# One pass over four heads for the state space products of a two-layer hybrid decoder kernel

## The chip, the cores and the metric

The kernel runs on one core of a Trainium2 chip. The metric is the device time of one execution in microseconds (us). The kernel before was timed in three runs: 1581.88, 1584.16 and 1584.36 us, median 1584.16 us. A separate, profiled execution took 1581.26 us.

## What is computed

Two decoder layers over 272 tokens (16 learned meta tokens, then 256) of width 2048. Each layer normalises its input, projects it once to all branch inputs, runs three branches (attention, a pooling mixer, and the state space part) and projects their outputs back. The part that the change touches is the chunked state space product of the reference:

```
cb = jnp.einsum('bclgn,bcsgn->bcgls', cm, bm)
y_diag = jnp.einsum('bcgrls,bcsgrp->bclgrp', cb[:, :, :, None] * lm, xdt)
...
y_off = jnp.einsum('bclgn,bcgrpn,bcgrl->bclgrp', cm, prev, jnp.exp(cs))
return (y_diag + y_off).reshape(b, tp, h, p)
...
y = y + d_skip.astype(jnp.float32)[:, None] * xs
yg = (y.reshape(b, t, SSD_WIDTH) * jax.nn.silu(z.astype(jnp.float32))).reshape(b, t, SSD_GROUPS, -1)
```

There are 32 heads of 64 channels in 4 groups of 8, and two chunks of 128 tokens besides the 16 meta tokens. `y_diag` is the product within a chunk (the chunk product), `y_off` what comes from the state ahead of the chunk (the state product).

## The kernel before, in words

Channels lie on partitions and tokens along the free dimension, so a tile holds 128 channels by 272 tokens. The large projections are done as three fp32r matmuls each (lines 244 to 246): weights are split into a high half `wh` (ScalarE, line 211) and a rest `wl` (VectorE, line 219), up to ten half tiles ahead of TensorE. One column block of 256 outputs is 96 such matmuls, in four quarters of 24.

All other work is written as generators that a `tick()` after each quarter moves on by one step. So the order of every engine's instructions is fixed when the program is built: the step of a generator lies on TensorE between two quarters of a projection. A `yield` puts off what follows by one quarter, and `until(key)` waits (while building) for another generator to have come past a point. The engines then run their queues in this order and wait for each other through semaphores alone.

The state space part goes group by group. The blocks of a group are `xs` (two of them), `BC`, and `z` (two of them). For each group:

- `post_xs` (two blocks of 256 channels): VectorE takes the projection out of PSUM (line 459, into `xpad`), ScalarE and VectorE do the convolution (lines 796 and 802), ScalarE the silu (806) and copies of the meta tokens (`xr`, 826), then TensorE transposes (`px`, lines 845 and 847) and VectorE and GpSimd scale (852, 855, 860) and ScalarE and VectorE split (864, 865).
- `post_BC` makes `H`, the state ahead of each chunk, and starts four `decay` generators. Each fills `M` for one pair of heads (the masked product of `cb` and `lm`; VectorE 935, ScalarE 941, GpSimd 948).
- `post_z` runs once for each z block, that is, for two pairs of heads (four heads). It takes the gate out of PSUM, waits for `M` of a pair `c`, yields once, and calls `ssd_y` for that pair; then the same for the second pair. After a further step VectorE adds and gates (988, 990), ScalarE squares (992), GpSimd sums (993, 1001 to 1003), TensorE sums over partitions (`pn`, 1007), VectorE and GpSimd make the root (1010 and `rsqrt_g`, lines 272 to 282), VectorE scales (1015) and the mix is split.
- `ssd_y` does one pair of heads. In layer 0 alone there are two 16-token matmuls for the meta tokens (961). Then come four chunk products, two heads by two chunks, with 64 columns of weights each, the two heads to the two halves of PSUM's partitions (966, `py`). Then two state products of 128 columns, one for each chunk (970, `ph`). VectorE scales `ph` into `yo` (972) and adds the skip term to `py` (973).

Layer 1 drops the meta tokens here (`t0` is 16), so it has no line 961.

The bank ring `aux` has four PSUM banks. `py` and `ph` take one bank each for every pair of heads.

The lines around the call, in `post_z`:

```
for c in (2 * j, 2 * j + 1):
    yield from until(f"M{g}_{c}")
    yield 1
    yo = yo or pair("yo")
    ssd_y(g, c, yo)
yield 1
```

Of the kernel before, what the change touches and what calls it, by code (L numbers as in the profile page):

```python
# [13 lines left out]
OP = mybir.AluOpType  # L14
# [4 lines left out]
P = 128  # L19
T = 272  # L20
# [8 lines left out]
PRE, POST, CW, CB, NW, PSC, DSK = 0, 16, 32, 128, 152, 168, 176  # L29
# [73 lines left out]
def hybrid(ctx: ExitStack, tc: tile.TileContext, I, out, dbg=None, layers=2):  # L103
# [15 lines left out]
    V, A, G, TE = nc.vector, nc.scalar, nc.gpsimd, nc.tensor  # L119

    def pair(name):
        return pr.tile([P, 2, T], F32, name=name, tag="pair")

    def aux(name):
        return psa.tile([P, 512], F32, name=name, tag="a")
# [36 lines left out]
    for l in range(layers):  # L162
# [10 lines left out]
        for i in range(4):  # L173

            if i < 3:
                j = seq.index(("i", l, [b[:2] for b in blocks].index(("pv", i + 1)), PLQ))
            else:
                j = seq.index(("o", l, 0, PLQ))
            seq.insert(j + 1, ("p", l, i, 0))

    hseq, j = [], 0
    while j < len(seq):
        n = 1 + NLEAD if seq[j][:2] == ("m", 0) else 1
# [86 lines left out]
    def rsqrt_g(y, v, t):  # L270

        G.tensor_scalar(y.bitcast(I32), v.bitcast(I32), -0.5, RSQ, op0=OP.mult, op1=OP.add)
        G.tensor_tensor(t, y, y, op=OP.mult)
        G.tensor_tensor(t, t, v, op=OP.mult)
        G.tensor_scalar(t, t, -1.0, K2, op0=OP.mult, op1=OP.add)
        G.tensor_tensor(y, y, t, op=OP.mult)
        G.tensor_tensor(t, y, y, op=OP.mult)
        G.tensor_tensor(v, t, v, op=OP.mult)
        G.tensor_scalar(t, v, K1 ** 4, -10.0 / 3 * K1 * K1, op0=OP.mult, op1=OP.add)
        G.tensor_tensor(t, t, v, op=OP.mult)  # L280
        G.tensor_scalar(t, t, KF, 5.0 * KF, op0=OP.mult, op1=OP.add)
        G.tensor_tensor(y, y, t, op=OP.mult)
# [72 lines left out]
    def layer(L, hs):  # L355
        t0 = 0 if L == 0 else NM
        last = L == layers - 1
        TQ = T - t0
        pa = par[:, L]
# [7 lines left out]
        def until(key):  # L367
            while key not in done:
                yield 1
# [84 lines left out]
        def dump_m(name, ap):  # L454
            if name in dbg:
                nc.gpsimd.dma_start(dbg[name][:, :, t0:], ap[:, :, t0:])
# [102 lines left out]
        def mix_out(mix, f, c0, n):  # L559

            m, c = mix
            A.copy(m[:, 0, c:c + n, c0:T], f)
            V.tensor_tensor(m[:, 1, c:c + n, c0:T], f, m[:, 0, c:c + n, c0:T].bitcast(F32), op=OP.subtract)
# [206 lines left out]
        def gate(ps, c0, key):  # L770
            g_ = pair("gate")
            evac_r(g_[:, :, c0:T], ps, 2, c0)
            done.add(("ev",) + key)
            yield 1
            A.activation(g_[:, :, c0:T], g_[:, :, c0:T], AF.Silu)
            yield 1
            return g_
# [173 lines left out]
                                op=OP.mult)  # L951
            done.add(f"M{g}_{c}")

        def ssd_y(g, c, yo):
            s = sd[g]
            M, H, csb, xdt, cT = s["M"], s["H"], s["csb"], s["xdt"], s["C"]
            py = aux("py")
            if t0 == 0:
                for j in range(2):
                    h = 2 * c + j  # L960
                    TE.matmul(py[64 * j:64 * j + 64, 0:16], xdt[0:16, 0, h], M[0:16, h, 0:16], start=True, stop=True)
            for b in range(2):
                sl = slice(16 + b * P, 144 + b * P)
                for j in range(2):
                    h = 2 * c + j
                    TE.matmul(py[64 * j:64 * j + 64, sl], xdt[:, 1 + b, h], M[:, h, sl], start=True, stop=True)
            ph = aux("ph")
            for b in range(2):
                sl = slice(16 + b * P, 144 + b * P)
                TE.matmul(ph[:, sl], H[:, b, 2 * c:2 * c + 2].rearrange("p h d -> p (h d)"), cT[:, sl],  # L970
                          start=True, stop=True)
            V.tensor_tensor(yo[:, c % 2, 16:], ph[:, 16:T], csb[:, 2 * c, 16:], op=OP.mult)
            V.scalar_tensor_tensor(s["yg"][:, c, t0:], s["x"][c // 2][:, c % 2, t0:],
                                   pa[:, DSK + 4 * g + c:DSK + 4 * g + c + 1], py[:, t0:T], op0=OP.mult, op1=OP.add)

        def post_z(i, ps):
            g, j = i // 2, i % 2
            zg = yield from gate(ps, t0, ("z", i))
            s = sd[g]
            yg = s["yg"]  # L980
            yo = None
            for c in (2 * j, 2 * j + 1):
                yield from until(f"M{g}_{c}")
                yield 1
                yo = yo or pair("yo")
                ssd_y(g, c, yo)
            yield 1
            V.tensor_tensor(yg[:, 2 * j:2 * j + 2, 16:], yg[:, 2 * j:2 * j + 2, 16:], yo[:, :, 16:], op=OP.add)
            ysl = yg[:, 2 * j:2 * j + 2, t0:]
            V.tensor_tensor(ysl, ysl, zg[:, :, t0:T], op=OP.mult)  # L990
            q = pair("ysq")
            A.activation(q[:, :, t0:], ysl, AF.Square)
            G.tensor_tensor(q[:, 0, t0:], q[:, 0, t0:], q[:, 1, t0:], op=OP.add)  # L993
            if j == 0:
                s["q"] = q
                done.add(f"q{g}")
                return
            done.add(f"y{g}")
            yield from until(f"q{g}")
            qs = pr.tile([P, 2, T], F32R, name="ysr", tag="pair")  # L1000
            G.tensor_tensor(qs[:, 0, t0:], q[:, 0, t0:], s["q"][:, 0, t0:], op=OP.add)
            G.tensor_tensor(q[:, 0, t0:], q[:, 0, t0:], s["q"][:, 0, t0:], op=OP.add)
            G.tensor_tensor(qs[:, 1, t0:], q[:, 0, t0:], qs[:, 0, t0:].bitcast(F32), op=OP.subtract)
            yield PNY
            pn = aux("pn")
            for k in range(2):
                TE.matmul(pn[:, t0:T], ones_r, qs[:, k, t0:], start=k == 0, stop=k == 1)
            yield 1
            v = s["q"][:, 0, t0:]
            V.tensor_scalar(v, pn[:, t0:T], 1.0 / 512, EPS, op0=OP.mult, op1=OP.add)  # L1010
            rg = q[:, 0, t0:]
            rsqrt_g(rg, v, q[:, 1, t0:])
            yield PGY
            for c in range(4):
                V.scalar_tensor_tensor(yg[:, c, t0:], yg[:, c, t0:], pa[:, NW + 4 * g + c:NW + 4 * g + c + 1], rg,
                                       op0=OP.mult, op1=OP.mult)
            dump_m(f"mixS{L}_{g}", yg)
            m = slots.tile([P, 2, 4, T], F32R, name=f"mixS{L}_{g}", tag=f"S{SS[g]}")
            mixS[g] = m
            yield 1  # L1020
            mix_out((m, 0), yg[:, :, t0:], t0, 4)
            done.add(f"mixS{g}")
# [50 lines left out]
        def post_pg(i, ps):  # L1073
# [6 lines left out]
            for c in range(2):  # L1080
# [5 lines left out]

        post = {"iq": post_iq, "k": post_k, "v": post_v, "q": post_q, "ag": post_ag,
                "xs": post_xs, "BC": post_BC, "z": post_z, "pv": post_pv, "pg": post_pg}

        def banks(ps):  # L1090
# [342 lines left out]
    h = hs  # L1433
    for L in range(layers):
        h = layer(L, h)
# [78 lines left out]
```

## Time and profile before

| | |
|---|---|
| profiled execution | 1581.26 us |
| its span in the trace | 1579.5 us |
| median of the three timed runs | 1584.16 us |
| TensorE (matmul) busy | 1540.3 us, 98% |
| VectorE busy | 1206.4 us, 76% |
| ScalarE busy | 884.6 us, 56% |
| GpSimd busy | 416.5 us, 26% |

The span runs from the first to the last instruction of the program; the execution's own time is 1.8 us more than it. A busy share is a share of the span. In the trace every fp32 matmul stands as two records (two passes); a fp32r matmul is one. Matmuls overlap in the pipeline, so what one costs TensorE is the distance from its start to the next start, not its duration.

### The profile page before, as it was taken

The numbers are of one execution on the slowest core, as the hardware profiler recorded it, in microseconds if no ns is written. First come the engines' busy times: TensorE is split into PE (matmuls) and PEld (weight loads), VectorE is DVE, ScalarE is ACT, GpSimd is POOL, SyncE is SP. The second block draws the span as 40 slices with busy tenths as digits, with TensorE's granted clock in tenths as the row PEclk, the third lists the DMA queues.
The fourth block names the chain that finished last, engine by engine and source line by source line (L and its number), as shares of the span: only waits on it lengthen the run. The fifth ranks groups of instructions, "written<-read, shape, count | busy, mean of one in ns | idle before, by whom it ended". The sixth has DMA issues, their size and how long they took to land. (4 is left out here: it accounts for less than half of the span.)

```text
span 1579.5 us, 31128 instructions
## 1 busy us (share of the span) xinstructions
PE 1540.3 (98%) x11788; PEld 1475.4 (93%) x11788; DVE 1206.4 (76%) x2217; ACT 884.6 (56%) x1663; POOL 416.5 (26%) x416
## 2 busy tenths in 40 slices
PE   7999999999999999999998999999999999999997
PEld 6899999999999999999998999999999999988886
DVE  7899777798989776545588998787989888764554
ACT  6455566656667444444455555666676565444542
POOL 3823342233342421000103314322333324200000
PEclk9999999999999999999999999999999999999999
DMA  6545445454544465565536454454545455566652
GB/s 232 204 146 174 138 135 180 143 189 136 188 172 154 130 207 169 191 217 176 171 108 230 152 173 157 149 188 148 197 153 181 174 162 164 190 225 207 208 188 93
DMA packets 78310, 272.44 MB, mean 172 GB/s; under 512 B 8848, under 2 KB 11984, under 8 KB 77136
## 3 DMA queue, kind: packets, MB, share of 16 engines
q1 hardware_dynamic: 78064, 270.39, 51.5%
q8 instruction: 92, 1.51, 0.4%
q14 instruction: 58, 0.48, 0.1%
q10 hardware_dynamic: 96, 0.07, 0.0%
HBM read 266.03 MB, written 4.40 MB: 171 GB/s over the span
## 5 line engine op out<-in xcount | busy, mean ns | idle before, releaser
L219 DVE TENSOR_TENSOR wl<-wr,wh 128x512 fp32r<-128x512 f32 (+1 forms) x952 | 712.7, 773 | 270.0 <-PE go L246 70.5
L211 ACT CAST wh<-wr 128x512 fp32r<-128x512 f32 (+1 forms) x952 | 564.6, 615 | 430.2 <-PE go L245 91.7
L244 PE MATMUL g0xs<-u,wh 128*128 128x272 f32 x256 | 74.8, 292 | 0.0
L244 PE MATMUL g1xs<-u,wh 128*128 128x272 f32 x256 | 74.6, 291 | 0.0
L244 PE MATMUL g0z<-u,wh 128*128 128x272 f32 x256 | 74.5, 291 | 0.0
L246 PE MATMUL go<-mixS,wl 128*128 128x272 f32 x256 | 74.1, 290 | 0.0
L246 PE MATMUL g0xs<-u,wl 128*128 128x272 f32 x256 | 74.1, 290 | 0.0
L246 PE MATMUL g0z<-u,wl 128*128 128x272 f32 x256 | 74.1, 290 | 0.0
L246 PE MATMUL g1xs<-u,wl 128*128 128x272 f32 x256 | 74.1, 289 | 0.0
L244 PE MATMUL go<-mixS,wh 128*128 128x272 f32 x256 | 74.0, 289 | 0.0
L245 PE MATMUL g1xs<-u,wh 128*128 128x272 f32 x256 | 73.7, 288 | 0.0
L245 PE MATMUL g0xs<-u,wh 128*128 128x272 f32 x256 | 73.7, 288 | 0.0
L245 PE MATMUL g0z<-u,wh 128*128 128x272 f32 x256 | 73.6, 288 | 0.0
L245 PE MATMUL go<-mixS,wh 128*128 128x272 f32 x256 | 73.6, 288 | 0.0
L244 PE MATMUL g1z<-u,wh 128*128 128x256 f32 x256 | 72.7, 284 | 0.0
L451 POOL TENSOR_TENSOR ropet<-ropet,rope 128x512 f32<-128x512 f32 (+2 forms) x20 | 33.2, 1661 | 147.7 <-PE ptr L483 66.1
L246 PE MATMUL g1z<-u,wl 128*128 128x256 f32 x256 | 71.7, 280 | 0.0
L245 PE MATMUL g1z<-u,wh 128*128 128x256 f32 x256 | 71.6, 280 | 0.0
L948 POOL TENSOR_TENSOR M<-M,cbm 128x512 f32<-128x512 f32 x32 | 45.9, 1434 | 93.4 <-ACT M L941 93.4
L802 DVE SCALAR_TENSOR_TENSOR xs<-xpad,par,xs 128x272 f32<-128x272 f32 x96 | 62.1, 712 | 0.0
L1262 POOL TENSOR_TENSOR acc<-acc,osq 128x544 f32<-128x544 f32 x6 | 8.2, 1370 | 168.8 <-ACT osq L1248 168.8
L266 PE MATMUL got<-wh,mixS 128*128 128x512 f32 x128 | 50.8, 397 | 0.0
(531 smaller groups left out, 5523.9 us busy)
## 6 DMA issues: line engine op xcount, KB each, us to landing
wr<-wi SPq DMA_DIRECT2D x334, 512.0 KB, 3.3
wr<-wo SPq DMA_DIRECT2D x128, 512.0 KB, 3.4
csb<-csd SPq DMA_DIRECT2D x8, 1088.0 KB, 8.4
x<-xT SPq DMA_DIRECT2D x8, 272.0 KB, 5.0
res<-xT SPq DMA_DIRECT2D x4, 544.0 KB, 6.0
h1d<-o SPq DMA_DIRECT2D x4, 544.0 KB, 7.7
wr<-plw SPq DMA_DIRECT2D x8, 256.0 KB, 2.6
hx<-h1d SPq DMA_DIRECT2D x8, 256.0 KB, 3.7
```

Source lines behind the costliest of these rows:

```text
L211: A.copy(hi, r[:, 2 * h:2 * h + 2])
L219: V.tensor_tensor(lo, r[:, 2 * h:2 * h + 2], his[i].bitcast(F32), op=OP.subtract)
L244: TE.matmul(o, w_h, u[:, 0, k, t1:T], start=first and k == 0, stop=False)
L245: TE.matmul(o, w_h, u[:, 1, k, t1:T], start=False, stop=False)
L246: TE.matmul(o, w_l, u[:, 0, k, t1:T], start=False, stop=last and k == 3)
L266: TE.matmul(o, m_h, hi, start=first, stop=False)
L451: G.tensor_tensor(t[:, :nch, c0:T], t[:, :nch, c0:T], bc(rope[:, b + 1:b + 2, c0:T], [P, nch, n]), op=OP.mult)
L802: V.scalar_tensor_tensor(dst[:, c], x[:, c, 13 + j:13 + j + T], w[:, j:j + 1], dst[:, c], op0=OP.mult, op1=OP.add)
L948: G.tensor_tensor(M[:, hh, 16:], M[:, hh, 16:], bc(cbm[:, None, 16:], [P, 2, 256]), op=OP.mult)
L1262: G.tensor_tensor(acc[:, :, t0:], acc[:, :, t0:], s[:, :, t0:], op=OP.add)
```

## The change

`ssd_y` now does a whole z block, that is, two pairs of heads in one call. The four state products stand first, then the eight chunk products, and in layer 0 the four products of the meta tokens last, in a bank of their own (`pym`). `ph` and `py` are one bank each for both pairs, laid out as two times 256 tokens, without the meta tokens. VectorE scales `ph` of both pairs in one instruction (line 976 now), and the skip term is one instruction for each pair (980), in layer 0 a further one for the meta tokens of each pair (982). `post_z` waits for `M` of both pairs, yields once and calls `ssd_y` once.

```
--- before.py
+++ after.py
@@ -951,39 +951,46 @@
                                 op=OP.mult)
             done.add(f"M{g}_{c}")
 
-        def ssd_y(g, c, yo):
+        def ssd_y(g, j, yo):
+
             s = sd[g]
             M, H, csb, xdt, cT = s["M"], s["H"], s["csb"], s["xdt"], s["C"]
-            py = aux("py")
+            ph, py = (aux(n).rearrange("p (c l) -> p c l", c=2) for n in ("ph", "py"))
+            cc = (2 * j, 2 * j + 1)
+            for c in cc:
+                for b in range(2):
+                    TE.matmul(ph[:, c % 2, b * P:b * P + P], H[:, b, 2 * c:2 * c + 2].rearrange("p h d -> p (h d)"),
+                              cT[:, 16 + b * P:144 + b * P], start=True, stop=True)
+            for c in cc:
+                for b in range(2):
+                    for h in (2 * c, 2 * c + 1):
+                        rows = slice(64 * (h % 2), 64 * (h % 2) + 64)
+                        TE.matmul(py[rows, c % 2, b * P:b * P + P], xdt[:, 1 + b, h], M[:, h, 16 + b * P:144 + b * P],
+                                  start=True, stop=True)
             if t0 == 0:
-                for j in range(2):
-                    h = 2 * c + j
-                    TE.matmul(py[64 * j:64 * j + 64, 0:16], xdt[0:16, 0, h], M[0:16, h, 0:16], start=True, stop=True)
-            for b in range(2):
-                sl = slice(16 + b * P, 144 + b * P)
-                for j in range(2):
-                    h = 2 * c + j
-                    TE.matmul(py[64 * j:64 * j + 64, sl], xdt[:, 1 + b, h], M[:, h, sl], start=True, stop=True)
-            ph = aux("ph")
-            for b in range(2):
-                sl = slice(16 + b * P, 144 + b * P)
-                TE.matmul(ph[:, sl], H[:, b, 2 * c:2 * c + 2].rearrange("p h d -> p (h d)"), cT[:, sl],
-                          start=True, stop=True)
-            V.tensor_tensor(yo[:, c % 2, 16:], ph[:, 16:T], csb[:, 2 * c, 16:], op=OP.mult)
-            V.scalar_tensor_tensor(s["yg"][:, c, t0:], s["x"][c // 2][:, c % 2, t0:],
-                                   pa[:, DSK + 4 * g + c:DSK + 4 * g + c + 1], py[:, t0:T], op0=OP.mult, op1=OP.add)
+                pym = aux("pym")[:, 0:32].rearrange("p (c l) -> p c l", c=2)
+                for c in cc:
+                    for h in (2 * c, 2 * c + 1):
+                        rows = slice(64 * (h % 2), 64 * (h % 2) + 64)
+                        TE.matmul(pym[rows, c % 2], xdt[0:16, 0, h], M[0:16, h, 0:16], start=True, stop=True)
+            V.tensor_tensor(yo[:, :, 16:], ph, csb[:, 4 * j:4 * j + 4:2, 16:], op=OP.mult)
+            for c in cc:
+                d = pa[:, DSK + 4 * g + c:DSK + 4 * g + c + 1]
+                x, y = s["x"][j][:, c % 2], s["yg"][:, c]
+                V.scalar_tensor_tensor(y[:, 16:], x[:, 16:], d, py[:, c % 2], op0=OP.mult, op1=OP.add)
+                if t0 == 0:
+                    V.scalar_tensor_tensor(y[:, 0:16], x[:, 0:16], d, pym[:, c % 2], op0=OP.mult, op1=OP.add)
 
         def post_z(i, ps):
             g, j = i // 2, i % 2
             zg = yield from gate(ps, t0, ("z", i))
             s = sd[g]
             yg = s["yg"]
-            yo = None
             for c in (2 * j, 2 * j + 1):
                 yield from until(f"M{g}_{c}")
-                yield 1
-                yo = yo or pair("yo")
-                ssd_y(g, c, yo)
+            yield 1
+            yo = pair("yo")
+            ssd_y(g, j, yo)
             yield 1
             V.tensor_tensor(yg[:, 2 * j:2 * j + 2, 16:], yg[:, 2 * j:2 * j + 2, 16:], yo[:, :, 16:], op=OP.add)
             ysl = yg[:, 2 * j:2 * j + 2, t0:]
```

Only these instructions move; on ScalarE, GpSimd and the DMA queues the order stays as it is. On TensorE, in the first group of layer 0, the second stop of the projection `xs` (block 2 of the layer, before its last quarter) read before as follows:

```order
L246 MATMUL g0xs_3925<-u_2_130,wl_3853 128x272
L961 MATMUL py<-M,xdt 64x16 x2
L966 MATMUL py<-M,xdt 64x128 x4
L970 MATMUL ph<-BC,H 128x128 x2
L961 MATMUL py<-M,xdt 64x16 x2
L966 MATMUL py<-M,xdt 64x128 x4
L970 MATMUL ph<-BC,H 128x128 x2
L244 MATMUL g0xs_3925<-u_3_131,wh_3851 128x272
```

And now, at the same place:

```order
L246 MATMUL g0xs_3925<-u_2_130,wl_3853 128x272
L962 MATMUL ph<-BC,H 128x128 x4
L968 MATMUL py<-M,xdt 64x128 x8
L975 MATMUL pym<-M,xdt 64x16 x4
L244 MATMUL g0xs_3925<-u_3_131,wh_3851 128x272
```

Before, a group had three stops: one pair a quarter earlier, two pairs here (the second pair of the first z block and the first pair of the second one), one pair a quarter later. Now it has two stops, here and a quarter later, each with the two pairs of one z block. Line numbers behind the change are 7 higher.

On VectorE, at the last stop of the same group, before (`xpad` is the start of the next group's chain):

```order
L988 TENSOR_TENSOR yg<-yg,yo 128x2x256
L990 TENSOR_TENSOR yg<-yg,gate 128x544
L972 TENSOR_TENSOR yo<-ph,csb 128x256
L973 SCALAR_TENSOR_TENSOR yg<-xs,par,py 128x272
L459 TENSOR_TENSOR xpad_118<-g0xs_3925,r_133 128x2x272
```

And now:

```order
L995 TENSOR_TENSOR yg<-yg,yo 128x2x256
L997 TENSOR_TENSOR yg<-yg,gate 128x544
L976 TENSOR_TENSOR yo<-ph,csb 128x2x256
L980 SCALAR_TENSOR_TENSOR yg<-xs,par,py 128x256
L982 SCALAR_TENSOR_TENSOR yg<-xs,par,pym 128x16
L980 SCALAR_TENSOR_TENSOR yg<-xs,par,py 128x256
L982 SCALAR_TENSOR_TENSOR yg<-xs,par,pym 128x16
L459 TENSOR_TENSOR xpad_118<-g0xs_3925,r_133 128x2x272
```

Ahead of the instruction that takes the next `xs` block out of PSUM there are now five instructions in place of two; in layer 1, without the meta tokens, three.

## Rows read from the trace of the kernel before

**Rows 1.** The page's part 1: busy time, share of the span, instructions

```profile
PE 1540.3 (98%) x11788; PEld 1475.4 (93%) x11788; DVE 1206.4 (76%) x2217; ACT 884.6 (56%) x1663; POOL 416.5 (26%) x416
```

**Rows 2.** The waits, TensorE: who waited for whom, us in total, times, longest us

```profile
PE px L845 <- ACT xr L826: 6.0, 6, 1.1
PE pn L1007 <- POOL ysr L1003: 0.4, 1, 0.4
```

**Rows 3.** Timeline, TensorE, one stop of layer 1: start us, us, what

```profile
1300.23 0.28 PE L245 MATMUL g1pv<-u,wh 128*128 128x258 f32 x1
1300.35 0.28 PE L246 MATMUL g1pv<-u,wl 128*128 128x258 f32 x1
1300.56 0.66 PE L966 MATMUL py<-M,xdt 128*64 128x128 f32 x8
1301.15 0.71 PE L970 MATMUL ph<-BC,H 128*128 128x128 f32 x4
1301.62 0.36 PE L244 MATMUL g1pg<-u,wh 128*128 128x256 f32 x1
1301.82 0.28 PE L245 MATMUL g1pg<-u,wh 128*128 128x256 f32 x1
```

**Rows 4.** The same stop, windows opened later: records still running, first one's start

```profile
1300.72 0.50 PE L966 MATMUL py<-M,xdt 128*64 128x128 f32 x6
...
1300.94 0.28 PE L966 MATMUL py<-M,xdt 128*64 128x128 f32 x2
...
1301.36 0.50 PE L970 MATMUL ph<-BC,H 128*128 128x128 f32 x3
...
1301.58 0.28 PE L970 MATMUL ph<-BC,H 128*128 128x128 f32 x1
```

**Rows 5.** Timeline, TensorE, the first stop of layer 0 (second row: window opened later)

```profile
296.69 0.29 PE L245 MATMUL g0xs<-u,wh 128*128 128x272 f32 x1
296.82 0.29 PE L246 MATMUL g0xs<-u,wl 128*128 128x272 f32 x1
297.04 0.29 PE L961 MATMUL py<-M,xdt 16*64 16x16 f32 x4
...
297.12 0.21 PE L961 MATMUL py<-M,xdt 16*64 16x16 f32 x2
...
297.26 0.66 PE L966 MATMUL py<-M,xdt 128*64 128x128 f32 x8
297.84 0.71 PE L970 MATMUL ph<-BC,H 128*128 128x128 f32 x4
298.52 0.29 PE L245 MATMUL g0xs<-u,wh 128*128 128x272 f32 x1
```

**Rows 6.** Timeline, TensorE, from the projection to a 128-column fp32 transpose, layer 1

```profile
1109.84 0.29 PE L246 MATMUL g1xs<-u,wl 128*128 128x272 f32 x1
1109.97 0.27 PE L845 MATMUL px<-cst,xr 128*128 128x128 f32 x1
```

**Rows 7.** Timeline, VectorE, last stop of layer 0's first group; idle before, releaser

```profile
308.98 0.42 DVE L972 TENSOR_TENSOR yo<-ph,csb 128x256 f32<-128x256 f32 x1 [0.85 <-PE ph L970]
309.32 0.48 DVE L973 SCALAR_TENSOR_TENSOR yg<-xs,par,py 128x272 f32<-128x272 f32 x1
309.73 0.71 DVE L459 TENSOR_TENSOR xpad<-g0xs,r 128x544 f32<-128x544 f32 x1
```

**Rows 8.** Timeline, GpSimd, ScalarE, TensorE: the chain to the next group's px

```profile
322.52 0.42 POOL L272 TENSOR_SCALAR ysq<-ysq 128x272 int32<-128x272 int32 x1 [4.94 <-DVE ysq L1010]
...
333.76 0.41 ACT L865 CAST xdd<-xr 128x256 fp32r<-128x256 f32 x1 [0.61 <-POOL xr L860]
...
335.11 0.33 PE L845 MATMUL px<-cst,xr 128*128 128x128 f32 x1 [1.12 <-ACT xr L826]
```

**Rows 9.** Timeline, TensorE, one 64-column fp32 matmul alone (two windows)

```profile
52.59 0.44 PE L486 MATMUL pik<-ikp,cst 128*64 128x272 f32 x1 [1.82 <-POOL ikp L452]
...
52.87 0.49 PE L486 MATMUL pik<-ikp,cst 128*64 128x272 f32 x1
```

## The prediction

> **What bounds the kernel now.** I read the busy shares first: TensorE's matmuls fill 98% of the span, no other engine more than 76% [rows 1]. So time is won where TensorE issues in fewer slots or waits less. The list of waits comes next: away from the kernel's start, the ones near this change are six waits of `px` for `xr`, together 6.0 us, and one wait of `pn`, 0.4 us [rows 2]. Neither is for the state space products themselves. So I looked at the timeline of TensorE where these products stand between two quarters of a projection, and took the distances of starts.
>
> One stop of layer 1 (one pair of heads) runs from the last projection matmul at 1300.35 to the second one after it at 1301.82, 1.47 us [rows 3]. Two of these slots are the projection's own, 0.12 each (1300.23 to 1300.35), so the stop costs 1.23. What would it cost at the steady pace? The records of `py` come in twos, and the second and the fourth two start at 1300.72 and 1300.94, so a two takes 0.11; the second and the fourth pass of `ph` start at 1301.36 and 1301.58, 0.11 each [rows 4]. Four twos and four passes are 0.88 us. The other 0.35 us is paid at two places. Going in, the second two starts 0.37 after the last projection matmul, where 0.12 + 0.11 = 0.23 would be steady: 0.14 lost. Going from `py` to `ph`, the second pass starts 0.42 after the last two, where 0.22 is steady: 0.20 lost. Leaving `ph` for the projection loses nothing: 1301.58 to 1301.82 is 0.24, the steady 0.11 + 0.12.
>
> A stop of layer 0 is 1.70 us long, 1.45 without the projection's two slots of 0.125 [rows 5]. Its work is 0.88 plus two twos of the 16-token products at 0.08 (297.04 to 297.12), 1.04. So 0.41 is lost: 0.09 going in (297.12 is 0.30 after 296.82, steady 0.125 + 0.08), 0.20 from `py` to `ph` as in layer 1, which leaves 0.12 from the 16-token products to the 128-token ones.
>
> What loses time is the change of the weights' shape, not fp32 as such: an fp32 transpose with 128 columns starts 0.13 after a projection matmul, against 0.12 to 0.125 steady [rows 6]. That is a loss of 0.01.
>
> **The change, part by part.** The number of matmuls stays: for each z block four state products, eight chunk products and, in layer 0, four meta products. What falls is the number of entries. Each layer has 16 pairs of heads, and now 8 stops of two pairs.
>
> *Layer 1.* A z block now costs 0.01 into `ph`, 8 x 0.11 = 0.88 for its passes, 0.14 into `py`, 8 x 0.11 = 0.88 for its twos, and the exit from `py` to the projection. That exit stands nowhere in the trace. The nearest row is the passage from `py` to `ph`, 0.20, which goes between the same two shapes; the smallest passage is 0.09, and I take 0.30 as the other end, as far above. Sum 2.11 against 2 x 1.23 = 2.46: 0.35 saved, 8 x 0.35 = 2.8 us. The ends of the exit give 2.0 to 3.7.
>
> *Layer 0.* The same 0.01 + 0.88 + 0.14 + 0.88, then into the 16-token products, four twos of 0.08 = 0.32, and out. Going from 128 to 16 tokens stands nowhere either; the way back costs 0.12, and for the exit I take 0.20 again. Sum 2.55 against 2.90: 0.35 saved, 2.8 us. With the two unknown passages free (0) or at 0.25 each a block costs 2.23 or 2.73, and the layer saves 5.4 or 1.4 us.
>
> *VectorE.* At the last stop of a group it idles 0.85 us for `ph`, then runs 972 and 973 (0.34 and 0.41 from start to start) and takes the next `xs` block out of PSUM at 309.73, 0.75 after the products [rows 7]. Now `ph` is complete while `py` still runs, about 1 us (0.14 + 0.88) longer. The double-width 976 costs at most two of 972, 0.68, and is hidden under `py`; without that cover it would add its 0.68. Behind `py` stand two of the 0.41 instructions, 0.82, and in layer 0 two 16-token ones between nothing and 0.41 each. The meta products run 0.44 us beyond `py` (0.12 + 0.32), under the first of these. So the next block leaves PSUM about 0.05 to 0.1 later, counted from the end of the products, than before in layer 1. In layer 0 with a third of 0.41 for the small ones it is about 0.7 after the products, as before; at the full 0.41 it is 0.45 later. I cost VectorE at nothing; the bad end is 3 groups x 0.45 = 1.4 us in layer 0.
>
> The Trainium skill (PSUM — Partial Sum Buffer, section on bank collisions) asks that engines be kept apart by whole bank and quadrant, not by address. Two pairs of heads now share the `py` bank, so by that rule the first skip-term instruction waits for the second pair's products too; with a bank for each it could start 0.44 us earlier, and the chain would gain at most that. The sum above already has the wait.
>
> *The chain behind it.* Why don't the six waits of `px` swallow the gain? In the first of them GpSimd's root waits for the `ysq` that VectorE takes from `pn`, starting at 322.52; ScalarE then waits for GpSimd's `xr` until 333.76; TensorE waits 1.12 us until 335.11 [rows 8]. Between 309.73 and there other engines set the pace, so what TensorE saves in that stretch would be lost. But the savings all lie ahead of 309.73, and this chain starts at the products: VectorE idles for them [rows 7]. If the products end 0.7 earlier (two stops), so does the chain, and the wait stays 1.1. `M`, the input of the chunk products, comes no later than before, because both stops that are left stand where a stop stood already. The wait of `pn` behaves in the same way.
>
> Sum: 2.8 + 2.8 = 5.6 us. The profiled execution took 1581.26, so it would take 1575.7. It lies 2.9 below the median of the three runs, 1584.16; against that median I get **1578.5 us**.
>
> **Rivals.**
>
> *The chain doesn't follow.* VectorE's work of the first z block is now nearer to that of the second, and if it comes late to the last stop, the chain to `px` starts when it did before. Then TensorE's 0.7 us is lost in each of the three groups of layer 0 with such a wait, and in three groups of layer 1 and the one with the wait of `pn`: 7 x 0.7 = 4.9, and 1584.16 - 0.7 = 1583.5 us remains. Against it: at the last stop VectorE has 0.85 us to spare [rows 7], and its work there grows only by what the block's second pair adds to 976 and 980. 13%, mostly as a part of the loss.
>
> *The loss goes with each pair of heads, not with each change of shape*, so that it is paid again within `py` when the second pair's weights come. Then nothing changes: 1584.2 us. Against it: the third and fourth two of `py` change heads and chunks and keep 0.11 [rows 4]. The Trainium skill (TensorEngine Tiling, Key Properties) says that a change of tiling mode drains the engine and a change of tile alone does not. By that rule the 5.6 us stand, by this rival nothing does; rows 3 and 6 agree with the rule. 4%.
>
> *Heads no longer run side by side* (slower). A 64-column product alone shows its two passes 0.28 us apart at 272 tokens [rows 9], while those of `py` start in twos [rows 4]: two heads share the array, each on its half of the columns. If neighbours in the new order no longer met on opposite halves, a z block's 16 passes would take 16 x 0.11 instead of 8 x 0.11, 0.88 more, and 16 blocks would cost 14 us, in all 14 - 5.6 = 8.5 us slower, 1592.7 us. It decides at the first two of `py`: starts in twos or one by one. Against it: the head is the innermost loop, and its even and odd numbers go to opposite halves. 3%.
>
> **How the numbers follow.** The forecast has 80%. Its own terms reach from 3.4 us (2.0 + 1.4) to 9.1 us (3.7 + 5.4) saved, that is 1575.1 to 1580.8; the rival of the chain, in part, reaches to about 1582. I give 1575.0 to 1582.0, which leaves out the full loss of the chain and the two other rivals. About 0.2% (3.2 us) is what a measurement of this kernel tells from no change. Faster by more: the forecast and a little of the chain's rival, 0.82. Within it: the rest of that rival and the second one, 0.15. Slower: the third, 0.03.
>
> **What the profile after would show.** One stop for each z block: about 2.1 us net in layer 1 and 2.55 in layer 0, with the `py` records still in twos 0.11 apart. The exit from `py` (layer 1) or `pym` (layer 0) to the second projection matmul some 0.2 over steady. The six `px` waits near 1.0 us each, within 0.2; if they have grown to 1.7, the chain did not follow. VectorE idle ahead of 976 or 980 at the last stop of each group. If the stops are as short as said and the time is not, look at the waits of `px`, `pb` and `pn`; if the stops are not, the unknown exits are where I was wrong.

## The result, and the profile after

The changed kernel takes 1575.74 us in the median of four runs (1573.18 to 1576.45), the kernel before 1584.17 (1581.88 to 1584.36). The ratio is 0.995, with an interval from 0.9936 to 0.9964: faster by 8.4 us, or 0.5%. The forecast said 5.6 less, 1578.5. The value lies within the range that was given (1575.0 to 1582.0), close to its lower end. The profiled execution after took 1573.18 us with a span of 1571.4, which is 8.1 less than the 1581.26 and the 1579.5 of before.

The busy shares of the kernel after, first part of the page:

```profile
PE 1533.9 (98%) x11788; PEld 1475.4 (94%) x11788; DVE 1204.8 (77%) x2217; ACT 884.7 (56%) x1663; POOL 417.5 (27%) x416
```

It answers to [rows 1]. No count differs on any engine (on VectorE, layer 0 gains as many instructions as layer 1 loses); TensorE is busy 6.4 us less with the same matmuls.

One stop of layer 1 after, in the timeline of TensorE (start, duration, what); the last row is from a window opened later, where only the last two records of `py` still run:

```profile
1089.99 0.29 PE L246 MATMUL g1xs<-u,wl 128*128 128x272 f32 x1
1090.12 1.05 PE L962 MATMUL ph<-BC,H 128*128 128x128 f32 x8
1091.10 1.09 PE L968 MATMUL py<-M,xdt 128*64 128x128 f32 x16
...
1092.35 0.29 PE L245 MATMUL g1xs<-u,wh 128*128 128x272 f32 x1
...
1091.91 0.28 PE L968 MATMUL py<-M,xdt 128*64 128x128 f32 x2
```

From 1089.99 to 1092.35 are 2.36 us. Less the projection's two slots of 0.125, the stop costs 2.11, where two stops of [rows 3] cost 2.46. It was forecast at 2.11. The exit from `py` is 0.20: from the last two at 1091.91 to 1092.35 are 0.44, of which 0.11 and 0.125 are the steady slots of that two and of a projection matmul. The `py` records still come in twos.

One stop of layer 0, the last of its first group; the last two rows are from windows opened later, where only the later records of `pym` are still listed:

```profile
305.08 0.29 PE L246 MATMUL g0xs<-u,wl 128*128 128x272 f32 x1
305.21 1.05 PE L962 MATMUL ph<-BC,H 128*128 128x128 f32 x8
306.19 1.09 PE L968 MATMUL py<-M,xdt 128*64 128x128 f32 x16
307.22 0.41 PE L975 MATMUL pym<-M,xdt 16*64 16x16 f32 x8
...
307.79 0.29 PE L245 MATMUL g0xs<-u,wh 128*128 128x272 f32 x1
...
307.30 0.33 PE L975 MATMUL pym<-M,xdt 16*64 16x16 f32 x6
...
307.36 0.26 PE L975 MATMUL pym<-M,xdt 16*64 16x16 f32 x3
```

From 305.08 to 307.79 are 2.71, so 2.46 without the two slots; the rows are rounded, and unrounded it is 2.45 in all eight stops, against 2.90 for two stops of [rows 5] and 2.55 in the forecast. The last two rows tell where most of the 0.10 is: from the first `pym` two to the second it is 0.08, as in [rows 5], but from there to the third only 0.06.

VectorE at the same stop, with its idle time before and what ended it in brackets:

```profile
306.30 0.69 DVE L976 TENSOR_TENSOR yo<-ph,csb 128x512 f32<-128x512 f32 x1 [0.16 <-PE ph L962]
307.34 0.48 DVE L980 SCALAR_TENSOR_TENSOR yg<-xs,par,py 128x256 f32<-128x256 f32 x1 [0.34 <-PE py L968]
307.73 0.23 DVE L982 SCALAR_TENSOR_TENSOR yg<-xs,par,pym 128x16 f32<-128x16 f32 x1
307.88 0.47 DVE L980 SCALAR_TENSOR_TENSOR yg<-xs,par,py 128x256 f32<-128x256 f32 x1
...
308.41 0.72 DVE L459 TENSOR_TENSOR xpad<-g0xs,r 128x544 f32<-128x544 f32 x1
```

It answers to [rows 7]. VectorE still waits here for TensorE, first for `ph`, then for `py`: the double 976 lies under `py`, and the 16-token instructions cost 0.15 from start to start, not 0.41. The next `xs` block leaves PSUM at 308.41, 0.62 after the second projection matmul behind the stop (307.79). Before it left at 309.73 [rows 7], 0.83 after that matmul, which TensorE's timeline of before has at:

```profile
308.90 0.29 PE L245 MATMUL g0xs<-u,wh 128*128 128x272 f32 x1
```

Relative to TensorE's own work the chain behind it therefore starts 0.2 us earlier. At its other end stands the next group's `px`:

```profile
333.80 0.33 PE L845 MATMUL px<-cst,xr 128*128 128x128 f32 x1 [0.92 <-ACT xr L826]
```

From 308.41 to 333.80 the chain takes 25.39 us; before it was 25.38, from 309.73 to 335.11 [rows 7, 8]. So all of the fall of this wait, from 1.12 to 0.92, is the earlier start. The waits of TensorE after (who for whom, total, times, longest):

```profile
PE px L845 <- ACT xr L826: 5.4, 6, 0.9
PE pn L1014 <- POOL ysr L1010: 0.3, 1, 0.3
```

In [rows 2] these were 6.0 and 0.4. A `pn` whose loss stands in no wait row has gained too, in layer 0's last group: from its start to the next projection matmul it was 0.56 before (530.70 to 531.26) and is 0.25 after (526.32 to 526.57).

Where did the time come from? In each trace I measured stretch A, from the first `xs` to the last `pg` matmul of layer 0, and B, the same of layer 1; after, A runs from the first to the second of these rows of TensorE's timeline:

```profile
220.62 0.29 PE L244 MATMUL g0xs<-u,wh 128*128 128x272 f32 x1
...
606.45 0.29 PE L246 MATMUL g0pg<-u,wl 128*128 128x272 f32 x1
```

| | A | B | px waits, layer 0 | layer 1 |
|---|---|---|---|---|
| before | 390.31 | 372.91 | 1.12 1.04 1.02 | 0.96 0.95 0.95 |
| after | 385.83 | 369.81 | 0.92 0.86 0.85 | 0.91 0.91 0.91 |
| difference | -4.48 | -3.10 | -0.55 | -0.13 |

The stops give 8 x 0.45 = 3.6 of A and 8 x 0.345 = 2.76 of B. The `px` waits give 0.55 and 0.13, `pn` 0.31 and 0.12. That is 4.46 and 3.01 of the 4.48 and 3.10. What is left of the 8.1 lies outside, 0.2 in the start of the span and 0.3 elsewhere.

A second set of runs of the same kernel, `after_again`, shows how well that repeats:

> The changed kernel once more, on the same chip as the run above, so that the two and the kernel before can be compared: about 1575.7 us.

Measured: median 1575.08, ratio 0.9949 [0.9937, 0.9962], A 385.87, B 369.82. The stretches agree to 0.04 us, while the first `xs` matmul starts at 222.85 instead of 220.62. So A and B tell tenths apart that the timed runs cannot, and I read the experiments by them.

### The profile page after: what moved, and what is told of

It is laid out like the page before. It is cut to its first block, busy times and chain, and to the rows that moved or that the text cites. A ratio compares the mean times of both kernels' runs of the same rounds, so it can differ in the third digit from the quotient of the medians.

```text
span 1571.4 us, 31133 instructions
## 1 busy us (share of the span) xinstructions
PE 1533.9 (98%) x11788; PEld 1475.4 (94%) x11788; DVE 1204.8 (77%) x2217; ACT 884.7 (56%) x1663; POOL 417.5 (27%) x416
## 4 chain that ended last, share of the span: by engine, by line
PE 79%; DVE 10%; POOL 5%; issue 3%; ACT 2%; DMA 1%; SPq 0%; DVEq 0%; ACTq 0%; POOLq 0%
DVE wl L219 4%; PE go L246 4%; PE go L244 4%; PE go L245 4%; PE got L268 4%; PE got L266 4%; PE got L267 4%; PE g0z L244 2%; PE g0z L246 2%; PE g0z L245 2%; PE g1z L244 2%; PE g1z L246 2%; PE g1z L245 2%; PE g0xs L244 2%; PE g1xs L244 2%
```

## The experiments

The theory: a change of the weights' shape costs a passage, and two pairs share what each paid before; the `px` and `pn` waits shrink because VectorE's chain starts earlier against TensorE's work. Rivals: the loss goes with each pair; the merged VectorE instructions or the banks give the gain; the two halves of `py` need their alternating order.

**Pair by pair** (`e1_pairwise`). The changed kernel, but with the passages of before:

```
             for c in cc:
                 for b in range(2):
                     TE.matmul(ph[:, c % 2, b * P:b * P + P], H[:, b, 2 * c:2 * c + 2].rearrange("p h d -> p (h d)"),
                               cT[:, 16 + b * P:144 + b * P], start=True, stop=True)
-            for c in cc:
                 for b in range(2):
                     for h in (2 * c, 2 * c + 1):
```

> Changed kernel, but within a stop the products go pair by pair: state products and chunk products of the first pair, then those of the second. Stops, banks, VectorE's instructions and their order stay. Theory (the gain is fewer changes of the weights' shape): each z block pays one passage from py to ph (0.20 us) and one from ph to py (0.14) more, 16 x 0.34 = 5.5 us over the changed kernel (1575.7), so about 1581 us; a stop of layer 1 is 2.46 us net instead of 2.11, the px waits stay near 0.9. Rival (fewer stops, or VectorE's merged instruction, make the gain): about 1575.7.

Measured: 1581.49 us, ratio 0.9984 [0.9975, 0.9994]; A 388.60, B 372.66. Timeline of TensorE, one stop of layer 1:

```profile
1089.54 0.29 PE L246 MATMUL g1xs<-u,wl 128*128 128x272 f32 x1
1089.66 0.60 PE L962 MATMUL ph<-BC,H 128*128 128x128 f32 x4
1090.20 0.66 PE L967 MATMUL py<-M,xdt 128*64 128x128 f32 x8
1090.79 0.71 PE L962 MATMUL ph<-BC,H 128*128 128x128 f32 x4
1091.43 0.66 PE L967 MATMUL py<-M,xdt 128*64 128x128 f32 x8
...
1092.25 0.28 PE L245 MATMUL g1xs<-u,wh 128*128 128x272 f32 x1
```

From 1089.54 to 1092.25 are 2.71, 2.46 net, just the price of before, although only one call issues the products. Against the changed kernel a block costs 0.345 more, and A and B are 2.77 and 2.85 longer, close to 8 x 0.345 = 2.76 each. With both pairs in one run of `py` the second pair pays nothing more; parted again, it pays. So the loss goes with the change of shape, and the rival of a loss for each pair falls. The `px` waits here are those of the changed kernel (0.85 to 0.92), so their fall doesn't hang on the shorter stops. Layer 0's block costs 2.80 here, 0.10 less than the 2.90 of before: the meta products already stand together, so that much of the gain is their own share.

**A bank for each pair** (`e2_own_banks`). TensorE's order as changed, banks and VectorE's instructions as before:

```
-            ph, py = (aux(n).rearrange("p (c l) -> p c l", c=2) for n in ("ph", "py"))
             cc = (2 * j, 2 * j + 1)
...
+            phs, pys = ([aux(n) for c in cc] for n in ("ph", "py"))
...
-            V.tensor_tensor(yo[:, :, 16:], ph, csb[:, 4 * j:4 * j + 4:2, 16:], op=OP.mult)
...
+            for c, ph in zip(cc, phs):
+                V.tensor_tensor(yo[:, c % 2, 16:], ph[:, 16:T], csb[:, 2 * c, 16:], op=OP.mult)
```

> Changed kernel, TensorE's order kept (four state products, eight chunk products, four meta products), but each pair has its own ph and py bank and VectorE's instructions are those of before (two of 972, two of 973, meta tokens within 973). Theory (shape): stops as in the changed kernel, 2.11 and 2.45 us net, and about 1575.7 us; the px waits change by 0.2 at most. Rival (VectorE's merged instruction or fewer banks make the gain): well over 1578 us, toward 1584.

Measured: 1574.98, ratio 0.9944 [0.9927, 0.996]; A 385.93, B 369.61, stops 2.45 and 2.11, the `px` waits 5.3 in all. Within 0.2 us in each stretch it is the changed kernel: the shared banks and the merged instructions have no larger share in the gain. Nor is it the change of bank that TensorE pays for in a passage: here the bank changes within `ph` and within `py` too, and the stop is as short. But VectorE does move. At a last stop of layer 1, `py` starts on TensorE at 1095.31, and VectorE's timeline goes on:

```profile
1096.02 0.92 DVE L979 SCALAR_TENSOR_TENSOR yg<-xs,par,py 128x256 f32<-128x256 f32 x2 [0.17 <-PE py L970]
1096.85 0.72 DVE L459 TENSOR_TENSOR xpad<-g1xs,r 128x544 f32<-128x544 f32 x1
```

In the changed kernel, at the stop of layer 1 shown first, `py` starts at 1091.10, and VectorE has:

```profile
1092.27 0.87 DVE L980 SCALAR_TENSOR_TENSOR yg<-xs,par,py 128x256 f32<-128x256 f32 x2 [0.37 <-PE py L968]
1093.06 0.71 DVE L459 TENSOR_TENSOR xpad<-g1xs,r 128x544 f32<-128x544 f32 x1
```

With a bank of its own the first pair's skip term starts 0.71 after `py` does, with a shared one 1.17: 0.46 earlier, where the prediction had 0.44 from the second pair's products. The Trainium skill (PSUM — Partial Sum Buffer, section on bank collisions) asks that engines be kept apart by bank and quadrant, not by address; these rows agree, as the first skip term waits for all that goes into its bank. The next block then leaves PSUM 0.42 earlier (1.54 against 1.96 behind the start of `py`). And yet the three waits of `px` in layer 1 are 0.91 in both kernels. From that block to `px` the chain takes 24.97 us in the changed kernel and 25.39 here. Of the 0.42, 0.13 is lost ahead of VectorE's reading of `pn`, and 0.29 in two instructions of GpSimd's root, which run longer. GpSimd in the changed kernel, then here:

```profile
1107.24 1.06 POOL L274 TENSOR_TENSOR ysq<-ysq 128x256 f32<-128x256 f32 x1
1110.02 1.04 POOL L277 TENSOR_TENSOR ysq<-ysq 128x256 f32<-128x256 f32 x1
...
1111.16 1.28 POOL L274 TENSOR_TENSOR ysq<-ysq 128x256 f32<-128x256 f32 x1
1114.16 1.11 POOL L277 TENSOR_TENSOR ysq<-ysq 128x256 f32<-128x256 f32 x1
```

Counted from the second projection matmul behind the stop (1092.35 and 1096.57), line 277 ends at 18.7 us in both. So an earlier start of this chain is worth nothing there any more. What holds GpSimd until then no run shows.

**State products first, nothing else** (`e3_state_first`). The kernel before with `ph` ahead of `py` in `ssd_y`; it keeps one passage for each pair:

```
+            ph = aux("ph")
+            for b in range(2):
+                sl = slice(16 + b * P, 144 + b * P)
+                TE.matmul(ph[:, sl], H[:, b, 2 * c:2 * c + 2].rearrange("p h d -> p (h d)"), cT[:, sl],
+                          start=True, stop=True)
             py = aux("py")
...
-            ph = aux("ph")
-            for b in range(2):
-                sl = slice(16 + b * P, 144 + b * P)
-                TE.matmul(ph[:, sl], H[:, b, 2 * c:2 * c + 2].rearrange("p h d -> p (h d)"), cT[:, sl],
-                          start=True, stop=True)
```

> Kernel before, pair by pair with its three stops in a group, only the state products moved ahead of the chunk products within ssd_y. Theory (shape): the passages are as many as before (in from ph 0.14 or 0.09, out of py 0.20), so stops cost 1.23 and 1.45 us as before; VectorE's yo now runs under py, which brings the chain to px forward by up to 0.34 us in seven groups, so 1581.8 to 1584.2 us, with px waits of 0.6 to 1.1. Rival (state products first, and not the merging, make the gain): about 1576 us.

Measured: 1581.41, ratio 0.9991 [0.9981, 1.0], which the timed runs alone don't tell from no change; stops 1.45 and 1.23 as before, A 0.80 and B 0.65 shorter. The waits of TensorE:

```profile
PE px L845 <- ACT xr L826: 5.3, 6, 0.9
```

No `pn` row near this change is left. The stops are what they were, so the 1.45 us by which A and B are shorter is the fall of the waits (0.75 at `px`, 0.6 at `pn`), and the order within a stop is enough for it. With `ph` last, the projection followed it free of loss while VectorE had both its instructions still ahead; with `py` last, TensorE pays the exit there, and VectorE's work on `ph` is done. The changed kernel gains about this and its shorter stops.

**Neighbours on the same half** (`e4_same_half`). In `py` the chunk becomes the innermost loop, so that two products on one half of the columns follow each other:

```
-                for b in range(2):
-                    for h in (2 * c, 2 * c + 1):
+                for h in (2 * c, 2 * c + 1):
+                    for b in range(2):
```

> Changed kernel, in the chunk products the chunk is the innermost loop instead of the head, so that two neighbours go to the same half of PSUM's partitions. Theory (two heads side by side on opposite halves): the twos of records break up, the 16 passes of a z block take 1.3 to 1.76 us instead of 0.88, 16 blocks cost 7 to 14 us, so 1583 to 1590 us. Rival (a 64-column product costs 0.11 us whatever stands beside it): no change, 1575.7 us.

Measured: 1575.45, ratio 0.9949 [0.9934, 0.9963]; A 386.17, B 370.24. Timeline of TensorE, a stop of layer 1:

```profile
1091.16 0.29 PE L246 MATMUL g1xs<-u,wl 128*128 128x272 f32 x1
...
1092.27 1.14 PE L968 MATMUL py<-M,xdt 128*64 128x128 f32 x16
...
1093.58 0.29 PE L245 MATMUL g1xs<-u,wh 128*128 128x272 f32 x1
```

A stop costs 2.42 - 0.25 = 2.17, 0.05 more than as changed, where serial passes would cost 0.88. My expectation was wrong: the order that I took for necessary is worth 0.05. The Trainium skill (TensorEngine Tiling, Key Properties) says that different tiles of the array run independently; this row agrees, as far as two products in succession go.

**One half after the other** (`e8_half_outermost`). How far does that reach? All four products of the lower half, then all of the upper:

```
-            for c in cc:
-                for b in range(2):
-                    for h in (2 * c, 2 * c + 1):
...
+            for k in range(2):
+                for c in cc:
+                    for b in range(2):
+                        h = 2 * c + k
...
```

> Changed kernel; the eight chunk products of a stop go first for the four heads-by-chunks of the lower half of PSUM's partitions, then for the upper half. With chunks innermost the stop had grown by 0.05 us only, so neighbours need not alternate. Theory A (work for the two halves overlaps only within a short reach): the halves run one after the other, up to 1.76 us in place of 0.88, 0.4 to 0.88 us for each of 16 blocks, 1582 to 1590 us. Theory B (the two halves run side by side over the whole stop, or a 64-column product costs 0.11 us alone): under 0.15 us for each block, 1575.7 to 1578 us; the records then show whether the two halves overlap in time.

Measured: 1582.92, ratio 1.0001 [0.9992, 1.001]; A 389.74, B 373.67. Timeline of TensorE, a stop of layer 1; the last two rows are from windows opened later:

```profile
1089.70 0.29 PE L246 MATMUL g1xs<-u,wl 128*128 128x272 f32 x1
...
1090.82 1.58 PE L968 MATMUL py<-M,xdt 128*64 128x128 f32 x16
...
1092.56 0.29 PE L245 MATMUL g1xs<-u,wh 128*128 128x272 f32 x1
...
1091.80 0.60 PE L968 MATMUL py<-M,xdt 128*64 128x128 f32 x4
...
1092.12 0.27 PE L968 MATMUL py<-M,xdt 128*64 128x128 f32 x1
```

A stop costs 2.61, 0.49 more than as changed, and all of the gain is gone. In the records the first four and the last four passes start one by one, mostly 0.11 apart (1091.80 to 1092.12 for the last four), and only the middle ones overlap. So the halves run side by side only when work for the other half stands at most a few products on. The third rival's mechanism exists; in the worst order tried it costs about half of the 0.88 that I gave it.

**Meta products over all rows** (`e5_meta_rows`, `e5_again`). The 16-token products take 16 rows of weights; here the same work goes over 128 partitions (the rows added hold zeros in effect, since `cbm` is masked), so that the rows no longer change from `py` to `pym`:

```
-                        TE.matmul(pym[rows, c % 2], xdt[0:16, 0, h], M[0:16, h, 0:16], start=True, stop=True)
+                        TE.matmul(pym[rows, c % 2], xdt[:, 0, h], M[:, h, 0:16], start=True, stop=True)
...
-                TE.matmul(pc[0:16, 256:272], bT[:, 0:16], cT[:, 0:16], start=True, stop=True)
+                TE.matmul(pc[:, 256:272], br, cT[:, 0:16], start=True, stop=True)
```

(and the same widening in the VectorE, ScalarE and GpSimd instructions on `cbm` and the meta part of `M`.)

> Changed kernel; in layer 0 the 16-token work keeps the shapes of its neighbours: M, cbm and the meta products span 128 partitions (rows beyond 16 are zero through the mask) and the meta part of cb uses the repeated meta tokens as 128 columns of weights. As many instructions, the same widths. Theory (a passage between shapes costs time): the 0.12 us from the chunk products into pym goes in 8 blocks, 0.8 to 1.0 us, and the stop of pc, 1.01 us net in layer 0 against 0.67 in layer 1, falls by 0.1 to 0.25 in four groups; in all 1.2 to 2.0 us, 1573.7 to 1574.5 us against 1575.7. Rival (narrow products cost what they cost, whatever their rows): stops of 2.45 and 1.01 us stay, 1575.7.

> The kernel of e5 once more, beside the two above: 1574 to 1575 us.

Measured: 1574.06, ratio 0.9949 [0.9936, 0.9961], and again 1575.38, 0.9951 [0.9939, 0.9964]; A 385.01 and 385.03. Timeline of TensorE, the first stop of layer 0's first group:

```profile
302.72 0.29 PE L246 MATMUL g0xs<-u,wl 128*128 128x272 f32 x1
...
303.83 1.09 PE L968 MATMUL py<-M,xdt 128*64 128x128 f32 x16
304.76 0.36 PE L975 MATMUL pym<-M,xdt 128*64 128x16 f32 x8
305.28 0.29 PE L245 MATMUL g0xs<-u,wh 128*128 128x272 f32 x1
```

From `py` to `pym` it is 0.93 where it was 1.03 (306.19 to 307.22), so the passage to 16 rows is nearly all gone; the block costs 2.31, 0.15 less. That is 1.2 us in the layer, and the stops of `pc`, widened too, give 0.4 more. But A fell by 0.8 only: the three `px` waits of layer 0 rose to about 1.0 each, 0.4 in all, and `pn` in its last group waits again, some 0.4. The trace tells why for `px`. At the last stop of the first group, TensorE's second projection matmul and VectorE's next block:

```profile
310.59 0.29 PE L245 MATMUL g0xs<-u,wh 128*128 128x272 f32 x1
...
311.36 0.72 DVE L459 TENSOR_TENSOR xpad<-g0xs,r 128x544 f32<-128x544 f32 x1
```

VectorE's four instructions begin when `py` is done and take as long as before, so the block leaves 0.77 behind that matmul, where it was 0.62. The 0.15 that TensorE gained isn't followed by the chain, which from there to `px` takes 25.3 us, much as before.

**All eight heads in one stop** (`e9_one_stop`). Both z blocks' products in one call, 16 passes of `ph`, then 32 of `py`:

```
-            for c in cc:
+            for c in range(4):
                 for b in range(2):
-                    TE.matmul(ph[:, c % 2, b * P:b * P + P], H[:, b, 2 * c:2 * c + 2].rearrange("p h d -> p (h d)"),
+                    TE.matmul(phs[c // 2][:, c % 2, b * P:b * P + P],
+                              H[:, b, 2 * c:2 * c + 2].rearrange("p h d -> p (h d)"),
                               cT[:, 16 + b * P:144 + b * P], start=True, stop=True)
...
+            if j == 0:
+                yield from until(f"yo{g}")
+                yo = s["yo"][0]
+            else:
+                for c in range(4):
+                    yield from until(f"M{g}_{c}")
+                yield 1
+                s["yo"] = [pair("yo") for _ in range(2)]
+                ssd_y(g, s["yo"])
```

> All eight heads of a group in one stop, at the place of the last stop: eight state products, sixteen chunk products, eight meta products, five banks in turn. Theory of the chain: TensorE saves a further set of passages in each group, 0.34 us in layer 1 and 0.45 in layer 0, 3.2 us in all; but VectorE's skip-term, add and gate instructions of the first z block now stand behind the products and ahead of the next block, 1.3 to 2.4 us, so the px waits grow from 0.9 to 2 to 3 us in six places, and the pn wait of the last group with them; about 1580 to 1586 us. Rival (fewer passages always win): about 1572.5 us with px waits as they are.

Measured: 1589.7, ratio 1.0047 [1.0031, 1.0062]; A 394.75, B 374.42, 8.9 and 4.6 more than as changed. The stops do what the theory says, 4.45 for a group where two stops cost 4.9, but the waits take it back many times. The waits of TensorE, the row for `pn`:

```profile
PE pn L1020 <- POOL ysr L1016: 11.1, 8, 1.9
```

The gating of the first z block now stands behind the same stop as that of the second, and GpSimd's sums come too late for `pn` in each group. I had expected the loss at `px`, 2 to 3 us each, and 1580 to 1586 us; the wait came at `pn`, and with the clock it cost more. Counted by the distance from the start before, in A the slots of `pn` grew by 8.7 us, while those of the state space products fell by 1.3 and those of `px` by 1.8. Another 3.1 went to projection matmuls, for the clock fell after the first two of these waits. The stretches of e9 (us, PE busy and count, PEld, VectorE, ScalarE, GpSimd, granted clock, DMA share, GB/s), and the row of the wait:

```profile
318.00:320.00 2.00, 0.81 (x5) 0.46 (x4) 2.00 (x3) 1.98 (x4) 1.84 (x3) 1.00 0.09 14
320.00:322.00 2.00, 1.49 (x8) 1.49 (x9) 2.00 (x5) 0.76 (x1) 0.46 (x1) 0.78 0.72 248
322.00:324.00 2.00, 2.00 (x11) 2.00 (x10) 2.00 (x4) 1.52 (x4) 0.00 (x0) 0.50 0.00 0
```

```profile
320.51 0.40 PE L1020 MATMUL pn<-ysr,ones 128*128 128x272 f32 x1 [1.71 <-POOL ysr L1016]
...
322.04 0.43 PE L245 MATMUL g0xs<-u,wh 128*128 128x272 f32 x1
322.26 0.43 PE L246 MATMUL g0xs<-u,wl 128*128 128x272 f32 x1
```

The clock of 0.50 is the lower level, 1.2 GHz; the matmuls then start 0.22 apart, not 0.125. This is the kind of loss that the first rival feared, at `pn` in place of `px`: the merging pays only as long as the engines behind keep up.

**Meta products first, over all rows, with own banks** (`e10_meta_first`). The edits of e2 and e5 together, with the `pym` loop moved between `ph` and `py`:

```
+            if t0 == 0:
+                for c, py in zip(cc, pys):
+                    for h in (2 * c, 2 * c + 1):
+                        rows = slice(64 * (h % 2), 64 * (h % 2) + 64)
+                        TE.matmul(py[rows, 0:16], xdt[:, 0, h], M[:, h, 0:16], start=True, stop=True)
+            for c, py in zip(cc, pys):
```

> The full-width meta products of e5 together with the banks and VectorE's instructions of e2 (a bank for each pair, meta tokens in the py bank), the meta products ahead of the chunk products. In e5 TensorE's stops of layer 0 were 0.29 us shorter in each group, but half of it came back as longer waits of px (1.00 to 1.02 against 0.85 to 0.92), because four VectorE instructions still stood behind the chunk products. Theory (the chain to px starts behind the products): with two instructions of 0.41 in place of four the chain starts 0.25 us earlier, the px waits of layer 0 fall back to 0.85 to 0.9, the pn wait of e5 in layer 0 (0.2) goes; stops stay near 2.30 net; TensorE from the first stop to the end of layer 0's state space part gains 0.5 to 0.9 us on e5; 1573 to 1574 us. Rival (the px waits are at a floor that other engines set): px waits stay at 1.0, no gain on e5.

Measured: 1574.08, ratio 0.9942 [0.9929, 0.9956], beside 1575.08 for the changed kernel on the same chip; A 384.46, B 369.54, so 1.4 and 0.3 less than as changed. The block of layer 0 costs 2.35, and the `px` waits of layer 0 fall back from e5's 1.0 to 0.86, as expected: the next block leaves PSUM 0.30 behind the second projection matmul, against 0.77 in e5. They don't fall below that, because from there to `px` the chain takes 25.65 us, 0.26 more than in the changed kernel. By the stretches it is the best of these kernels, about 1.7 us below the changed one; the intervals overlap, so the timed runs don't tell the two apart.

## Why the prediction was right, point by point

- **Layer 1, 2.11 against 2.46: right.** It measured 2.11, and the exit from `py`, which no row of before showed, is 0.20. Taking the passage from `py` to `ph` for it was the right choice. 2.8 us said, 2.76 found.
- **Layer 0, 2.55 against 2.90: right in kind, 0.10 too dear.** The step that was mis-sized is "four twos of 0.08". The 0.08 was the one distance that [rows 5] had, and that is the first after a change of shape; the later ones are 0.06. The sum said 2.8 us, it is 3.6.
- **"I cost VectorE at nothing": wrong, by a gain.** I counted when the next block leaves PSUM from the end of the products, and there it is nearly as said. But TensorE's second projection matmul now comes 0.13 (layer 0) to 0.20 (layer 1) later behind the last product because of the exit, where there was no such loss behind `ph`. Against TensorE's work the chain starts earlier, and the waits fell by 1.1 us in all (0.68 at `px`, 0.43 at `pn`). e3 has that part alone, without any merging: 1.45 in the two stretches. For `px` the start of the chain accounts for it (25.38 and 25.39 us from there on); `pn` I did not follow up in this way. It goes no further than 0.85 to 0.92 for each wait, as e2 shows in layer 1 and e10 in layer 0.
- **The chain follows: right.** The `px` waits are 0.85 to 0.92, not 1.7, with VectorE idle ahead of 976 and 980. In e9, where the chain does not follow, the kernel is slower than before.
- **The sum.** 5.6 was said. 0.8 for the meta products and 1.1 for the waits were missed, which makes 7.5; the rest up to 8.1 in the profiled executions lies nearly all outside the two layers' stretches. That the time still fell within the range is in part luck: the range's lower end stood for cheaper exits, but the exits cost what was said, and a term sized too dear and one put at nothing took that room.
- **The rivals.** Loss for each pair: fell with e1. The halves in series: didn't happen; e4 shows that alternation is hardly needed, e8 that the mechanism is real at about half of its price. The Trainium skill's rule (TensorEngine Tiling, Key Properties) that a change of mode drains the engine and a change of tile does not agrees with e1 and the stops after: eight products of `py` pay one entry and one exit, and what that costs here is 0.14 and 0.20. The rows show the price, not that it is a drain.

Open: what lengthens GpSimd's lines 274 and 277 when the chain starts earlier, and so holds the `px` waits at 0.85 to 0.92 in kernels as different as e2, e3 and e10. No run was made to tell.

## What to carry to other kernels

Count how often the weights' shape changes between neighbouring matmuls, and gather the work of one shape into one stretch: here an entry and an exit of 64-column weights cost some 0.35 us, whether four or eight products stand between. Gather only as far as the engines behind can still start their work in time, and look for the wait that grows; four heads in one go paid, eight did not. Put last in such a stretch what the other engines have least to do for, and take a distance right behind a change of shape for what it is, not for the steady pace.

## What I had not expected of the hardware

- Two products on opposite halves of the columns need not be neighbours to run side by side: with two on one half in succession a stop loses 0.05 us (e4), with four in succession 0.49 (e8).
- After two waits of 1.71 us of TensorE in e9 the granted clock fell to 0.50; after three others of 1.70 to 1.94 us in the same execution, and after the `px` waits of about 1 us in all runs, it did not. The length of the wait doesn't tell them apart: after a wait of 2.17 us of `pik` in layer 1 it fell to 0.50 in the trace of the changed kernel and stayed at 1.00 in that of `after_again`, the same kernel. What does was not tried.
- The time at which the first `xs` matmul starts scatters between 220.6 and 223.9 us over the executions, though no kernel differs ahead of it, while A repeats to 0.04 us. The scatter of the timed runs of one kernel (1580.98 to 1585.23 for the one before) is of like size.
